# Split weights of the input projections: low part by a negation on GpSimd and an accumulating DMA in place of a subtraction

## The chip, the cores and the metric

The kernel runs on one core of a Trainium2 chip. It is one launch for both layers of a small model and two request groups. The metric is the device time of an execution in microseconds (us), taken as the median of several runs. Five engines work beside each other: TensorE (PE, matmuls, with PEld for the loads of its weights), VectorE (DVE), ScalarE (ACT), GpSimd (POOL) and SyncE (SP, which here only issues DMAs). Each runs its own list of instructions in order and waits on semaphores for the others; 16 DMA engines move data.

## The reference

Each of the two layers adds the output of three mixers and then a feed-forward part to x. All three mixers read slices of one combined projection `h @ w_in`, 1024 to 2600 columns.

```
def layer(x, ...):
    h = rms_norm(x, g_mix)
    z = h @ w_in                                   # 1024 x 2600
    za, zb, q, k, v, qi, ki, wi = split(z)
    y_a = u * (W_s v + b)       of gelu(za)        # mixer A: spatial gate over chunks of 128
    y_b = gb * conv3(gc * h_in) of zb              # mixer B: causal convolution of width 3
    y_c = attention over the top-k keys that the indexer (qi, ki, wi) picks   # mixer C
    x = x + concat(y_a, y_b, y_c) @ w_out
    hf = rms_norm(x, g_ffn)
    return x + relu(hf @ w_up) ** 2 @ w_down
```

Inputs are 512 rows of a new stream and 32 rows of a running one with 1024 cached keys, all in float32. Beside y, the new keys, values, indexer keys and states of the two request groups are outputs.

## The kernel before

**Products in three passes.** A float32 product is made of float32r matmuls, a format that PE takes in one pass. Every operand is split into a high part `hi` (the value rounded to float32r) and a low part `lo` (what is missing), and `mm3` adds hi x hi, hi x lo and lo x hi. For weights this is done by `load_w`, for activations by `split`.

**Loading weights.** `load_w` takes 1024 weight columns in a partition at a time (592 for the indexer): SP loads them as they are into `raw` (two buffers), ACT writes `hi` (line 216), and DVE or POOL writes `lo = raw - hi` (line 217). `hi` and `lo` lie in a ring of 3072 columns each, which is three blocks: the high part of a block can be written when PE has ended the block three before it. The engine for line 217 is DVE unless the caller names POOL with `nc.gpsimd`.

**The input projections.** In both layers the order in the source is: the indexer (line 353, 296 columns in four blocks), Q in two groups, K, V and mixer A's v (256 columns each, in two blocks: rows 0 to 511 and 512 to 1023 of the weights), then mixer A's u and mixer B's three groups (`w_feat`, 128 columns a block, two blocks each). The 256-column groups are products with tokens as output rows (`tok_gemm`): each of five token blocks has 24 matmuls, the first 12 with the group's first weight block, the last 12 with its second. For the first token block, line 377 also multiplies the sample's rows by `raw` itself. In the 128-column groups (`fm_gemm`) a weight block has two halves of 24 matmuls.

**Who sets the order.** A list scheduler turns the source into one list for each engine, by priorities (`prep` for weights, `evac` for copies out of PSUM) and its own idea of how long things take. So the same source lines come in another order when an operation changes. What lies beside the projections is work for DVE and ACT: rotary tables (lines 396 to 398), squares and norms (lines 596 to 648), the indexer's scores (lines 546 to 550), the search of the top-k (lines 405 to 456) and the softmax. Line 380 is ACT's copy of the sample's part product out of PSUM; line 644 begins the norm of a K block.

**POOL's list.** It holds the subtractions of the indexer's blocks of layer 1, of Q, V and mixer A's u, copies of the sample's normed rows (line 261), the tables of the next layer, the first three blocks of `w_up`, and the issues of small stores (line 511 indexer keys, 650 keys, 669 values).

Of the kernel before, what the change touches and what calls it, by code (L numbers as in the profile page):

```python
# [25 lines left out]
# column groups of w_in  # L26
# [5 lines left out]
# scheduling priorities of weight loads and of copies out of PSUM  # L32
PREP = -1000000
EVAC = -2000000
# columns of the ring of split weights
# [3 lines left out]
class Shift:  # L39
    """Shifts the scheduling priority of what is traced inside."""  # L40
# [12 lines left out]
def kernel(  # L53
# [45 lines left out]
    def tr(out, in_, ident):  # L99
        """A transpose on TensorE, which moves the bits as they are (float32r in one pass)."""  # L100
        if in_.dtype == F32R:
            out = out.bitcast(F32R)
        nc.tensor.transpose(out, in_, ident)  # L103
# [20 lines left out]
    # per-feature vectors as columns: g_mix, g_ffn, conv_w, state_conv  # L124
# [23 lines left out]
    def rsqrt_newton(r, s, scale, shape_like):  # L148
        """r = (s * scale) ** -0.5, the table's value with one Newton step; s may lie in PSUM."""
        r0 = shape_like()  # L150
        nc.scalar.activation(r0, s, AF.Abs_reciprocal_sqrt, scale=scale)
        u = shape_like()
        nc.vector.scalar_tensor_tensor(u, s, -0.5 * scale, r0, op0=ALU.mult, op1=ALU.mult)
        nc.vector.tensor_tensor(u, u, r0, op=ALU.mult)
        nc.vector.scalar_tensor_tensor(r, u, 1.5, r0, op0=ALU.add, op1=ALU.mult)
# [3 lines left out]
    def take_x(h, tags):  # L159
        """A half of x to feature-major, and the norm's factors along the rows' columns."""  # L160
        blocks = (0, 1) if h == 0 else (2, 3, 4)
        nb = len(blocks)
        size = lambda b: 128 if b < 4 else NS
        s, r = sm(nb, "sa", 6), sm(nb, "sa", 6)
        nc.vector.memset(s, 1.0)
        for i, b in enumerate(blocks):
            n = size(b)
            nc.scalar.activation(junk[:n, i % 2], xin[b][:n], AF.Square, accum_out=s[:n, i:i + 1])
        nc.vector.tensor_scalar(s, s, EPS * D, None, op0=ALU.add)
        rsqrt_newton(r, s, 1.0 / D, lambda: sm(nb, "sr"))  # L170
        rst[h] = T(HALF[h])
        pr = psum("d")
        for i, b in enumerate(blocks):
            n = size(b)
            for g in range(2):
                p = psum(next(tags))
                for k in range(4):
                    tr(p[:, k * n:k * n + n], xin[b][:n, (4 * g + k) * 128:(4 * g + k + 1) * 128], idn[:n, :n])
                dst = xs[h][:, 4 * g:4 * g + 4, i * 128:i * 128 + n]
                src = p[:, :4 * n].rearrange("p (k n) -> p k n", k=4)  # L180
                if g == 0:
                    nc.vector.tensor_copy(dst, src)
                else:
                    nc.scalar.copy(dst, src)
        for i, b in enumerate(blocks):
            n = size(b)
            dr = T(128, "tt")
            nc.vector.tensor_scalar(dr[:n, :n], idn[:n, :n], r[:n, i:i + 1], None, op0=ALU.mult)
            nc.tensor.matmul(pr[:, i * 128:i * 128 + n], lhsT=ones[:n, :], rhs=dr[:n, :n], start=True, stop=True)
        nc.vector.tensor_copy(rst[h], pr[:, :HALF[h]])  # L190
# [11 lines left out]
    ring = [wp.tile([128, RING], F32R, name="hi"), wp.tile([128, RING], F32R, name="lo"), 0]  # L202

    def load_w(fill, a, c, eng=None):
        """a row blocks of weights, c columns each: two float32r parts that sum to them exactly, and they themselves."""
        with prep:
            raw = rawp.tile([128, a, c], F32, tag="raw", name=nm("raw"))
            if callable(fill):
                fill(raw)
            else:  # L210
                nc.sync.dma_start(raw, fill.rearrange("(k p) c -> p k c", p=128))
            if ring[2] + a * c > RING:
                ring[2] = 0
            hi, lo = (t[:, ring[2]:ring[2] + a * c].rearrange("p (k c) -> p k c", k=a) for t in ring[:2])
            ring[2] += a * c
            nc.scalar.copy(hi, raw)  # L216
            (eng or nc.vector).tensor_tensor(lo, raw, hi.bitcast(F32), op=ALU.subtract)  # L217
        return [(hi[:, k], lo[:, k], raw[:, k]) for k in range(a)]
# [11 lines left out]
    # the sample's normed rows, not split  # L230
    hraw = const.tile([128, 8, 32], F32, name="hraw")

    def add_square(h, m):
        """Adds the squares of block m of x to the half's sum (with the eps share of a partition)."""
        n = HALF[h]
        t = T(n)
        nc.scalar.activation(t, xs[h][:, m, :], AF.Square)
        if m == 0:
            ssq[h] = keep([128, n], f"work{h + 1}")
            nc.vector.tensor_scalar(ssq[h], t, EPS * D / 128, None, op0=ALU.add)  # L240
        else:
            nc.vector.tensor_tensor(ssq[h], ssq[h], t, op=ALU.add)  # L242
# [21 lines left out]
    def results(b, g, tag):  # L264
        """A block's output, half of its features, back to token-major."""
# [15 lines left out]
    def prepare(l):  # L281
# [42 lines left out]
    def search_constants():  # L324
# [3 lines left out]
        # for the threshold search: prefix sums, the copies' total, steps  # L328
# [15 lines left out]
    for l in range(depth):  # L344
# [8 lines left out]
        idxw += w_tok(C_IDX, 296, ((2, 4), (4, 6), (6, 8)), nc.gpsimd if l else None)  # L353
# [11 lines left out]
        def tok_gemm(b, pieces, n, aside=True):  # L365
            """Token-major product of a block; aside: the sample's rows by themselves, in float32."""
# [5 lines left out]
            if b == 0 and aside:  # L372
                # the sample's rows: parts of the sum side by side in the array's columns
# [17 lines left out]
        def rope(t1, t2, x, ca, sb, half):  # L391
            """t1 = x * cos, t2 = swapped x * sin; x [rows, j, h, e] in PSUM."""
# [8 lines left out]
        def topk_mask(work, n, rounds, tag):  # L401
            """Turns scores into 0 where taken and NEG elsewhere."""
# [6 lines left out]
        def sample_mask(x):  # L409
            """The same for the sample's scores, whose rows are there four times (rows 32 j + t).  # L410

            The k-th largest score is found digit by digit (two bits of its float's exponent or mantissa at a
            time, each copy of a row trying one digit); equal scores are taken in the order of the keys.
            """
# [4 lines left out]
            # sign of the k-th largest; which one of sgn * x it is  # L419
# [7 lines left out]
            def digit(nb):  # L427
                """How many candidates of a row at least kk of sgn * x reach (a tie at the candidate counts half)."""
# [29 lines left out]
            # a tie at the last candidate may have hidden it: count exactly there  # L458
# [10 lines left out]
            # prefix counts of the equal ones  # L469
# [8 lines left out]
            # as many of them as are missing: k - (sum of signs + n - equal) / 2  # L478
# [15 lines left out]
        for b in range(5):  # L494
# [58 lines left out]
            else:  # L553
# [5 lines left out]
                # w as two [(head, t), (copy, t)] matrices  # L559
# [47 lines left out]
        for u in range(2):  # L607
            pieces = w_tok(C_Q + 256 * u, 256, ((0, 4), (4, 8)), nc.gpsimd)
            for b in range(5):
# [5 lines left out]
                # columns (j, hh, e) to (hh, j, e)  # L615
# [15 lines left out]
        pieces = w_tok(C_K, 256, ((0, 4), (4, 8)))  # L631
# [28 lines left out]
        pieces = w_tok(C_V, 256, ((0, 4), (4, 8)), nc.gpsimd)  # L660
# [18 lines left out]
        def attend(b):  # L679
            """The block's steps of a pair of query heads: scores and softmax, then the values."""  # L680
# [3 lines left out]
            def scores(u, hh):  # L684
                # two key heads side by side: their scores in halves of the array's rows
# [21 lines left out]
            def values(u, hh, probs, po):  # L707
                for k0 in range(0, b + 1, 2):
# [7 lines left out]
                    # and their values in halves of its columns  # L716
# [16 lines left out]
        def attend_sample():  # L733
# [17 lines left out]
            # queries, scaled  # L751
# [43 lines left out]
        def fm_gemm(h, src, ws, k0=0):  # L795
            """Feature-major product of a half: the weights' columns are the output's rows."""
            p = psum("m")
            n = HALF[h]
            for i, w in enumerate(ws):
                mm3(p[:, :n], w, (src[h][0][:, k0 + i, :], src[h][1][:, k0 + i, :]), i == 0, i == len(ws) - 1)  # L800
            return p
# [7 lines left out]
        def mixers():  # L809
# [1 line left out]
            mixT = [T(2 * n, "g").rearrange("p (h n) -> p h n", h=2) for n in HALF]  # L811
            pieces = w_tok(C_VA, 256, ((0, 4), (4, 8)))
# [27 lines left out]
            for fb in range(2):  # L840
                wt = w_feat(C_U + 128 * fb, nc.gpsimd)
# [8 lines left out]
            for fb in range(2):  # L850
                gc = T(NT + NS, "g")
                wt = w_feat(C_GC + 128 * fb)
# [9 lines left out]
                wt = w_feat(C_H + 128 * fb)  # L862
# [13 lines left out]
                wt = w_feat(C_GB + 128 * fb)  # L876
# [39 lines left out]
        def heat(h, m):  # L916
            """Has ScalarE's table for the norm loaded before its first use."""
# [70 lines left out]
def _constants():  # L988
    """Identity and rotary tables: they depend on shapes alone."""
# [13 lines left out]
    # the sum over the copies 1..3 of a row  # L1003
# [41 lines left out]
```

## Time and profile before

| | |
|---|---|
| three runs | 1397.32, 1400.68, 1401.14 us; median 1400.68 |
| span of the profiled execution (the page gives no other time of it) | 1403.4 us |
| mean granted TensorE clock | 0.982 |
| busy: PE / PEld / DVE / ACT / POOL | 1353.1 / 1265.8 / 840.0 / 615.9 / 115.3 us |
| weight blocks: high part on ACT | 188 |
| low part on DVE / on POOL | 163 / 25 |
| DMA bytes, mean rate | 113.00 MB, 81 GB/s |

The input projections and attention of layer 0 stand at 10 to 250 us of the span, those of layer 1 at 700 to 940 us. What lies after each is the output projection and the feed-forward part. An engine's busy time says little by itself here; the waits inside one stage are what is read.

### The profile page before, as it was taken

Reading aid. Unit: us, or ns where it says so; the run is one execution under the profiler, and the core shown is the slowest. Engines: PE = TensorE matmul, PEld = TensorE weight load, DVE = VectorE, ACT = ScalarE, POOL = GpSimd, SP = SyncE. Lnnn points to the kernel's source line nnn. Section 1 sums busy time; section 2 is a strip of 40 time slices with the busy share of each in tenths; the row PEclk is TensorE's granted clock in tenths of the full one; section 3 lists DMA queues with packets and bytes.
Section 4 is the critical chain, followed back from the end, with each engine's and each line's share of the span. In section 5 each row is a group of like instructions: output and inputs, shape, how many; then the busy total and the mean of one; then the engine's idle time right before and its main releaser. Section 6 shows DMA issues by size and latency. Waiting matters only on the chain. (4 is left out here: it accounts for less than half of the span.)

```text
span 1403.4 us, 25751 instructions
## 1 busy us (share of the span) xinstructions
PE 1353.1 (96%) x10430; PEld 1265.8 (90%) x10430; DVE 840.0 (60%) x2103; ACT 615.9 (44%) x1212; POOL 115.3 (8%) x125
## 2 busy tenths in 40 slices
PE   7998999998999999999989899999899999999998
PEld 5877886898999999999987789779799999999998
DVE  6999987468434334334489999865853343443442
ACT  5746996335314224223246489842542231331321
POOL 4414200010000000000042120000200000000000
PEclk8999999999999999999988999999999999999999
DMA  7124221323233332333212222222233332233322
GB/s 185 33 71 106 68 64 48 94 68 89 81 88 91 91 84 84 89 91 91 64 49 62 58 81 77 76 61 61 61 95 88 91 91 86 82 90 91 91 81 74
DMA packets 183566, 113.00 MB, mean 81 GB/s; under 512 B 7028, under 2 KB 180616, under 8 KB 183448
## 3 DMA queue, kind: packets, MB, share of 16 engines
q1 hardware_dynamic: 180808, 106.35, 26.2%
q0 software_dynamic: 2640, 5.01, 1.8%
q8 instruction: 82, 1.34, 0.4%
q14 instruction: 36, 0.29, 0.1%
HBM read 106.67 MB, written 4.67 MB: 79 GB/s over the span
## 5 line engine op out<-in xcount | busy, mean ns | idle before, releaser
L216 ACT CAST hi<-raw 128x1024 fp32r<-128x1024 f32 (+1 forms) x188 | 194.1, 1032 | 404.6 <-PE psm L226 389.1
L217 DVE TENSOR_TENSOR lo<-raw,hi 128x1024 fp32r<-128x1024 f32 (+1 forms) x163 | 197.5, 1212 | 174.9 <-ACT hi L216 174.2
L908 DVE TENSOR_TENSOR x<-x,psm 128x256 f32<-128x256 f32 (+1 forms) x192 | 83.7, 437 | 232.4 <-PE psm L227 232.0
L226 PE MATMUL psm<-h1lo,hi 128*128 128x288 f32 x640 | 190.4, 298 | 0.9 <-DVE h1lo L222 0.9
L227 PE MATMUL psm<-a1hi,lo 128*128 128x288 f32 x640 | 190.0, 297 | 0.0
L226 PE MATMUL psm<-a1lo,hi 128*128 128x288 f32 x640 | 189.9, 297 | 0.0
L225 PE MATMUL psm<-a1hi,hi 128*128 128x288 f32 x640 | 189.8, 297 | 0.0
L225 PE MATMUL psm<-h1hi,hi 128*128 128x288 f32 x640 | 188.7, 296 | 1.1 <-ACT h1hi L221 1.1
L227 PE MATMUL psm<-h1hi,lo 128*128 128x288 f32 x640 | 189.1, 296 | 0.0
L226 PE MATMUL psm<-h0lo,hi 128*128 128x256 f32 x640 | 181.9, 285 | 6.2 <-DVE h0lo L222 6.2
L225 PE MATMUL psm<-a0hi,hi 128*128 128x256 f32 x640 | 183.0, 286 | 0.0
L226 PE MATMUL psm<-a0lo,hi 128*128 128x256 f32 x640 | 182.0, 284 | 0.0
L227 PE MATMUL psm<-a0hi,lo 128*128 128x256 f32 x640 | 182.0, 284 | 0.0
L225 PE MATMUL psm<-h0hi,hi 128*128 128x256 f32 x640 | 181.4, 284 | 0.0
L227 PE MATMUL psm<-h0hi,lo 128*128 128x256 f32 x640 | 180.0, 282 | 0.0
L226 PEld LDWEIGHTS psm<-h0lo,hi 128*128 128x128 f32 x640 | 120.4, 188 | 8.6 <-DVE h0lo L222 7.1
L225 PEld LDWEIGHTS psm<-h1hi,hi 128*128 128x128 f32 x640 | 120.1, 188 | 2.7 <-ACT h1hi L221 1.5
L225 PEld LDWEIGHTS psm<-a0hi,hi 128*128 128x128 f32 x640 | 121.6, 190 | 0.5 <-issue 0.5
L226 PEld LDWEIGHTS psm<-h1lo,hi 128*128 128x128 f32 x640 | 120.3, 188 | 1.8 <-DVE h1lo L222 1.3
L226 PEld LDWEIGHTS psm<-a0lo,hi 128*128 128x128 f32 x640 | 121.2, 189 | 0.6 <-issue 0.5
L225 PEld LDWEIGHTS psm<-h0hi,hi 128*128 128x128 f32 x640 | 120.6, 189 | 1.2 <-issue 0.9
L227 PEld LDWEIGHTS psm<-a0hi,lo 128*128 128x128 f32 x640 | 121.6, 190 | 0.0
(318 smaller groups left out, 2841.1 us busy)
## 6 DMA issues: line engine op xcount, KB each, us to landing
raw<-in_w_up_dram SPq DMA_DIRECT2D x64, 512.0 KB, 4.1
raw<-in_w_down_dram SPq DMA_DIRECT2D x64, 512.0 KB, 3.9
raw<-in_w_in_dram SPq DMA_DIRECT2D x36, 512.0 KB, 3.9
raw<-in_w_out_dram SPq DMA_DIRECT2D x8, 512.0 KB, 3.8
raw<-in_w_out_dram SPq DMA_DIRECT2D x32, 128.0 KB, 3.0
raw<-in_w_in_dram SPq DMA_DIRECT2D x8, 296.0 KB, 6.1
q<-in_cache_k_dram SPq DMA_DIRECT2D x4, 512.0 KB, 4.3
h1lo<-in_cache_v_dram SPq DMA_DIRECT2D x2, 1024.0 KB, 7.1
```

Source lines behind the costliest of these rows:

```text
L216: nc.scalar.copy(hi, raw)
L217: (eng or nc.vector).tensor_tensor(lo, raw, hi.bitcast(F32), op=ALU.subtract)
L225: nc.tensor.matmul(out, lhsT=st[0], rhs=mv[0], start=first, stop=False)
L226: nc.tensor.matmul(out, lhsT=st[0], rhs=mv[1], start=False, stop=False)
L227: nc.tensor.matmul(out, lhsT=st[1], rhs=mv[0], start=False, stop=last)
L908: nc.vector.tensor_tensor(xs[h][:, m, :], xs[h][:, m, :], p[:, :HALF[h]], op=ALU.add)
```

## The change

For the input projections, the argument `eng` of `load_w` becomes the word "dma". Then POOL writes `lo = -hi`, and a DMA that POOL issues adds `raw` to what stands in `lo`. This is done for 39 blocks: in both layers Q (4), K, V and mixer A's v (2 each), u and mixer B's groups (8 in all), and in layer 1 the last three blocks of the indexer. Of these, 19 were subtracted on POOL and 20 on DVE before. The first layer's indexer, `w_out`, `w_up` and `w_down` stay as they are.

```
             hi, lo = (t[:, ring[2]:ring[2] + a * c].rearrange("p (k c) -> p k c", k=a) for t in ring[:2])
             ring[2] += a * c
             nc.scalar.copy(hi, raw)
-            (eng or nc.vector).tensor_tensor(lo, raw, hi.bitcast(F32), op=ALU.subtract)
+            if eng == "dma":
+
+                nc.gpsimd.tensor_scalar(lo, hi.bitcast(F32), -1.0, None, op0=ALU.mult)
+                nc.gpsimd.dma_start(lo, raw, accum_op=ALU.add)
+            else:
+                (eng or nc.vector).tensor_tensor(lo, raw, hi.bitcast(F32), op=ALU.subtract)
...
-        idxw += w_tok(C_IDX, 296, ((2, 4), (4, 6), (6, 8)), nc.gpsimd if l else None)
+        idxw += w_tok(C_IDX, 296, ((2, 4), (4, 6), (6, 8)), "dma" if l else None)
...
-            pieces = w_tok(C_Q + 256 * u, 256, ((0, 4), (4, 8)), nc.gpsimd)
+            pieces = w_tok(C_Q + 256 * u, 256, ((0, 4), (4, 8)), "dma")
...
-        pieces = w_tok(C_K, 256, ((0, 4), (4, 8)))
+        pieces = w_tok(C_K, 256, ((0, 4), (4, 8)), "dma")
...
-        pieces = w_tok(C_V, 256, ((0, 4), (4, 8)), nc.gpsimd)
+        pieces = w_tok(C_V, 256, ((0, 4), (4, 8)), "dma")
...
-            pieces = w_tok(C_VA, 256, ((0, 4), (4, 8)))
+            pieces = w_tok(C_VA, 256, ((0, 4), (4, 8)), "dma")
...
-                wt = w_feat(C_U + 128 * fb, nc.gpsimd)
+                wt = w_feat(C_U + 128 * fb, "dma")
...
-                wt = w_feat(C_GC + 128 * fb)
+                wt = w_feat(C_GC + 128 * fb, "dma")
...
-                wt = w_feat(C_H + 128 * fb)
+                wt = w_feat(C_H + 128 * fb, "dma")
...
-                wt = w_feat(C_GB + 128 * fb)
+                wt = w_feat(C_GB + 128 * fb, "dma")
```

The rest of the diff drops comments. Lines behind 217 have numbers higher by five after the change, so 226 becomes 231 and 511 becomes 516. The raw buffer of a block is now free when its accumulating DMA has landed.

POOL's list in layer 0 where Q begins, before: `raw_217_869` and `raw_218_873` are Q's first two blocks, `t_118_567` to `t_172_771` the indexer keys of token blocks 2 to 4.

```order
L217 TENSOR_TENSOR lo_163<-raw_217_869,hi_162 128x1024
L511 DMA out_4_dram<-t_118_567 128x32
L511 DMA out_4_dram<-t_145_669 128x32
L217 TENSOR_TENSOR lo_163<-raw_218_873,hi_162 128x1024
L513 DMA out_8_dram<-t_172_771 32x32
```

The same place of POOL's list after; `raw_218_874` is Q's second block, and a row `lo<-hi` is the negation of the block that the next DMA into `lo` adds.

```order
L219 TENSOR_SCALAR lo_163<-hi_162 128x1024
L516 DMA out_4_dram<-t_118_567 128x32
L220 DMA lo_163<-raw_217_869 128x1024
L219 TENSOR_SCALAR lo_163<-hi_162 128x1024
L516 DMA out_4_dram<-t_145_669 128x32
L220 DMA lo_163<-raw_218_874 128x1024
L518 DMA out_8_dram<-t_172_771 32x32
```

A block has two rows instead of one, and the issue of each add stands behind the store of an indexer key, of token block 2 for the first and 3 for the second.

PE's list at the same place before, from Q's first matmul to its first on a low part; line 544 is the indexer's score.

```order
L225 MATMUL psm_221_888<-hi_162,h0hi_28_184 128x256
L544 MATMUL psl_103_506<-kiTp_65_325,q_97_487 128x256
L226 MATMUL psm_221_888<-lo_163,h0hi_28_184 128x256
L544 MATMUL psl_107_516<-kiTp_65_325,q_97_487 128x256
L227 MATMUL psm_221_888<-hi_162,h0lo_29_185 128x256
```

And after:

```order
L230 MATMUL psm_221_890<-hi_162,h0hi_28_184 128x256
L549 MATMUL psl_103_506<-kiTp_65_325,q_97_487 128x256
L549 MATMUL psl_107_516<-kiTp_65_325,q_97_487 128x256
L230 MATMUL psm_225_924<-hi_162,h0hi_28_184 128x256
L230 MATMUL psm_229_958<-hi_162,h1hi_53_279 128x256
L549 MATMUL psl_109_521<-kiTp_65_325,q_97_487 128x256
L549 MATMUL psd_111_526<-kiTp_65_325,q_97_487 128x256
L549 MATMUL psl_113_531<-kiTp_65_325,q_97_487 128x256
L549 MATMUL psl_115_536<-kiTp_65_325,q_97_487 128x256
L231 MATMUL psm_221_890<-lo_163,h0hi_28_184 128x256
```

Eight matmuls stand between the first high and the first low part now, where one stood; among them the first matmuls of the next two token blocks.

PE's list in layer 0 where K's first token block (`psm_276`) comes from the first weight block to the second, before: the last of the first 12 matmuls, and the first two of the last 12.

```order
L227 MATMUL psm_276_1248<-hi_162,h0lo_29_185 128x256
L225 MATMUL psm_276_1248<-hi_162,h0hi_28_184 128x256
L226 MATMUL psm_276_1248<-lo_163,h0hi_28_184 128x256
L227 MATMUL psm_276_1248<-hi_162,h0lo_29_185 128x256
L225 MATMUL psm_276_1248<-hi_162,h0hi_28_184 128x256
```

And after; `psm_284` is the second token block:

```order
L230 MATMUL psm_276_1254<-hi_162,h0hi_28_184 128x256
L230 MATMUL psm_284_1300<-hi_162,h0hi_28_184 128x256
L231 MATMUL psm_284_1300<-lo_163,h0hi_28_184 128x256
L232 MATMUL psm_284_1300<-hi_162,h0lo_29_185 128x256
L230 MATMUL psm_284_1300<-hi_162,h0hi_28_184 128x256
L231 MATMUL psm_284_1300<-lo_163,h0hi_28_184 128x256
L232 MATMUL psm_284_1300<-hi_162,h0lo_29_185 128x256
L231 MATMUL psm_276_1254<-lo_163,h0hi_28_184 128x256
```

Six matmuls of the second token block, which need the first weight block alone, now stand ahead of the first use of the second block's low part.

## Rows read from the trace of the kernel before

**Rows 1.** Page, busy us of each engine, share of the span, instructions

```profile
PE 1353.1 (96%) x10430; PEld 1265.8 (90%) x10430; DVE 840.0 (60%) x2103; ACT 615.9 (44%) x1212; POOL 115.3 (8%) x125
```

**Rows 2.** Table by stage: start:end, length, busy us (instructions), clock, DMA share, GB/s

```profile
80.00:120.00 40.00, 35.97 (x274) 31.08 (x273) 37.53 (x131) 17.85 (x42) 8.54 (x9) 0.97 0.23 70
...
640.00:700.00 60.00, 60.00 (x479) 60.00 (x479) 27.38 (x51) 19.63 (x37) 0.00 (x0) 1.00 0.28 81
```

**Rows 3.** PE's waits, 40 to 200 us: total us, times, longest us

```profile
PE psm L225 <- ACT t L380: 2.9, 2, 2.4
PE psl L544 <- ACT t L546: 2.4, 1, 2.4
PE psx L103 <- DVE sr L644: 1.6, 1, 1.6
PE psl L103 <- ACT t L546: 1.4, 1, 1.4
```

**Rows 4.** PE's waits, 690 to 870 us

```profile
PE psm L225 <- ACT t L380: 2.8, 2, 2.3
PE psx L252 <- DVE work L242: 2.2, 1, 2.2
PE psl L544 <- ACT q L540: 2.0, 1, 2.0
PE psx L103 <- DVE sr L644: 2.0, 1, 2.0
PE psd L544 <- ACT t L546: 1.6, 1, 1.6
PE psl L103 <- DVE q L561: 1.1, 1, 1.1
```

**Rows 5.** Table by stage, a stretch at a granted clock of 0.50

```profile
118.01:121.42 3.41, 3.41 (x18) 3.41 (x18) 3.24 (x22) 2.40 (x4) 1.67 (x4) 0.50 0.41 136
```

**Rows 6.** Timeline of POOL, 103 to 118 us: start, us, instruction, [idle before]

```profile
112.38 2.37 POOL L217 TENSOR_TENSOR lo<-raw,hi 128x1024 fp32r<-128x1024 f32 x1
```

**Rows 7.** Timeline of DVE, 103 to 118 us

```profile
103.18 0.41 DVE L641 TENSOR_TENSOR t<-t,t 128x256 f32<-128x256 f32 x1
...
112.16 2.88 DVE L641 TENSOR_TENSOR t<-t,t 128x256 f32<-128x256 f32 x1
```

**Rows 8.** Groups of instructions, DVE: busy us, mean ns of one, idle before

```profile
L217 DVE TENSOR_TENSOR lo<-raw,hi 128x1024 fp32r<-128x1024 f32 (+1 forms) x163 | 197.5, 1212 | 174.9 <-ACT hi L216 174.2 <-DMA raw<-in_w_out_dram 0.5
```

**Rows 9.** Groups of instructions, POOL, shapes apart

```profile
L217 POOL TENSOR_TENSOR lo<-raw,hi 128x1024 fp32r<-128x1024 f32 x22 | 53.1, 2415 | 353.3 <-ACT hi L216 349.3 <-PE psl L103 3.9
...
L332 POOL CAST tri<-q 128x640 bf16<-128x640 f32 x1 | 0.8, 817 | 3.6 <-DMA q<-in_c_tri_dram 3.6
...
L338 POOL CAST idb<-idr 128x128 bf16<-128x128 f32 x1 | 0.3, 302 | 0.0
```

**Rows 10.** DMA issues: KB each, median us from issue to landing

```profile
raw<-in_w_down_dram SPq DMA_DIRECT2D x64, 512.0 KB, 3.9
...
h1lo<-in_cache_v_dram SPq DMA_DIRECT2D x2, 1024.0 KB, 7.1
...
out_dram<-t POOLq DMA_DIRECT2D x8, 128.0 KB, 2.0
```

**Rows 11.** Page, DMA queue: packets, MB, share of 16 engines

```profile
q1 hardware_dynamic: 180808, 106.35, 26.2%
```

**Rows 12.** Timeline of ACT, 93.5 to 101 us

```profile
95.98 1.03 ACT L216 CAST hi<-raw 128x1024 fp32r<-128x1024 f32 x1
```

**Rows 13.** Timeline of PE, 93.5 to 101 us

```profile
94.80 0.28 PE L227 MATMUL psm<-hi,h1lo 128*128 128x256 f32 x1
...
99.94 0.28 PE L226 MATMUL psm<-lo,h0hi 128*128 128x256 f32 x1
```

**Rows 14.** Timeline of POOL, 44 to 54 us

```profile
46.57 1.22 POOL L511 DMA_DIRECT2D out_dram<-t  x2
```

**Rows 15.** Timeline of PE, 46 to 53.5 us

```profile
47.27 0.28 PE L226 MATMUL psm<-lo,h0hi 128*128 128x256 f32 x1
```

## The prediction

> **What bounds the kernel now.** I read the page's busy times first, then the table by stage, then who waits for whom on TensorE (PE), then the timeline around the longest waits. The reader is to see in the first that PE is busy for 1353.1 us [rows 1], so all its idle time in a span of 1403.4 us is 50 us. The table by stage shows where that time isn't: in the feed-forward part PE is busy for 60.00 of 60 us and issues a matmul every 60/479 = 0.125 us, while at 80 to 120 us, in the input projections that the change touches, it has 35.97 of 40, with VectorE (DVE) at 37.53 [rows 2]. There DVE is the engine behind PE's waits, directly or through ScalarE (ACT): 2.4, 1.4, 1.6 and a 2.4 of the 2.9 in the first layer [rows 3], and 2.2, 2.0, 2.0, 1.6, 1.1 and most of 2.8 in the second [rows 4]. That is about 20 us over both layers, and it is nearly all that a change to these stages can win from waits. A gap also costs clock: after the wait that ends at 116.8 us PE has a granted clock of 0.50 for 3.41 us, that is the 1.2 GHz level [rows 5]. Such a window takes 3.41/2 = 1.7 us of PE's work, and there is one behind most of these waits.
>
> What makes DVE late is not its own subtractions but those of GpSimd (POOL). The timeline of DVE has one and the same instruction (line 641) at 0.41 us and at 2.88 us; the long one stands beside a subtraction on POOL that runs from 112.38 for 2.37 us [rows 6, 7]. DVE instructions on two SBUF operands stop while POOL subtracts. The waits of rows 3 and 4 follow such stops by 1 to 5 us.
>
> **The change part by part.** Changed are 39 blocks of input-projection weights: 18 in layer 0 and 21 in layer 1. 19 of them were subtracted on POOL, 20 on DVE. In a block two steps now stand where one stood: POOL writes the negated high part, and an accumulating DMA, issued by POOL, adds the raw block to it.
>
> *Removed from DVE:* 20 subtractions of 1.212 us [rows 8], 24 us. I cost this at nothing. In these stages each such block now gives DVE a hold by POOL's negation in exchange, and where PE is saturated (after 160 us of a layer) a faster DVE helps nobody.
>
> *On POOL:* the subtraction of 1024 columns takes 2.415 us, a one-input copy of 640 columns 0.817 and one of 128 columns 0.302 [rows 9]. So (0.817-0.302)/512 = 1.01 ns a column, and the negation is 0.302+896 x 1.01 ns = 1.21 us (estimate). The bounds are this and the two-input 2.415. I take 1.21, since the copies too have one input. A hold of DVE gets shorter by 2.37-1.21 = 1.16 us, if a one-input instruction holds DVE at all, which no row shows apart: the gain of a place lies between nothing (it holds as long as before) and 2.37 (it doesn't hold).
>
> The Trainium skill (SBUF — State Buffer, Who interferes with whom) says that a DVE instruction with two SBUF inputs contends with a GpSimd instruction that reads SBUF, and that the second to issue is blocked until the first ends. By this the trace agrees for the subtraction, and the negation, which reads SBUF, would hold DVE for its own length; so the page speaks for 1.16 and against 2.37.
>
> Of the waits in rows 3 and 4, seven shrink: 1.4, 1.6 and 2.4 (for line 380) in layer 0, 2.0 (for line 644), 2.3 (of the 2.8 for line 380), 1.6 and 1.1 in layer 1. Seven times 1.16, the last at its 1.1: -8.1 us. In layer 1 the three 592-column blocks of the indexer stood in the norm that PE waits for (2.2 [rows 4]); scaled by columns, 3 x 1.16 x 592/1024 = -2.0.
>
> *The new latency.* Today the low part is there one subtraction after the high part. Now it is: negation 1.2, semaphore 0.1, then issue to landing of an accumulating SBUF-to-SBUF DMA of 512 KB. No row has one. Loads of 512 KB land in 3.9 us and of 1024 KB in 7.1, and a store of 128 KB from POOL's queue in 2.0 [rows 10]. The bounds are 3.9 (as a plain copy) and 7.1 (it moves what 1024 KB move, since it has to read the old destination as well). In between: all hardware-queue packets moved 106.35 MB in 26.2% of 16 engines' span [rows 11], so an engine moves 106.35 MB/(0.262 x 16 x 1403.4 us) = 18 GB/s. A store of 128 KB has 8 KB an engine; two reads of 512 KB have 64 KB an engine, 56 KB or 3.1 us more, on top of 2.0: 5.1 us. I take 5.1 (estimate); it is nearer to 3.9.
>
> The Trainium skill (Collectives: The Full Stack, The bandwidth ceiling) says that an add inside a DMA engine is slow not for the add but because it needs two source reads, at half the rate of a copy. No run here shows it. [...]
>
> Where does that meet PE? The ring holds three blocks. In mixers and projections of 128 columns two blocks of 48 matmuls lie between a freed slot and the first use: 2 x 48 x 0.125 = 12 us, against 0.1 (semaphore)+1.05 (high part)+0.1+1.2+0.1+5.1 = 7.7. Covered; this cover is gone from a landing of 9.4 on. Later raw loads are covered in the same way, since a raw buffer is free 5 us later and the load itself takes 4 of those 12. Not covered are the second blocks of the 256-column groups. K in layer 0: the slot is freed at 95.08 (94.80+0.28), the high part is made from 95.98 to 97.01, the low part is first used at 99.94 [rows 12, 13]. Now: negation to 98.3, issue 98.4, landing 103.5. The new order puts the use some 0.7 us later (six matmuls of the next token block stand in between), 100.65. So PE waits 2.85 us, and again in layer 1, where the order is the same: +5.7. The second blocks of V and of mixer A have the wait for line 380 or some attention work in between, which makes them 2 to 3 us longer; I put +1.0 for the four.
>
> At the start of Q the accumulating DMA stands in POOL's queue behind the store of an indexer key. That store was issued at 46.57 [rows 14], held up by the subtraction; with 1.1 us less hold and 0.6 for the issue, the add is issued at 46.1 and lands at 51.2. PE used the low part at 47.27 [rows 15] and has eight matmuls put ahead of it, so it wants it at 48.6 and waits 2.6. The wait of 2.4 that stood 4 us later (layer 1: 2.0) goes in return, since DVE and ACT catch up meanwhile: +0.2 and +0.6, +0.8 in all. Behind the waiting add nothing stands on POOL that PE needs sooner.
>
> **Sum.** -8.1 -2.0 +5.7 +1.0 +0.8 = -2.6 us. Half-clock windows I leave at zero: two or three should go with the shorter waits, as many come with those at K and Q. The sum is made in the profiled execution, of which the page tells the span alone, 1403.4 us; the three runs have a median of 1400.68, 2.7 less, so I take the sum off that: 1398 us.
>
> **Rivals.** *The add is dear.* If it lands in 7.1 us or later (1024 KB did [rows 10]), the eight uncovered second blocks and Q starts wait 2.0 us longer each, +16, and four or so of them are then long enough for a half-clock window of 1.7 us of lost work: +4 to +25, about 1418, slower. It decides from a landing of 6 us on. For it: the operation reads twice and no row shows it. Against: rows of 4 KB in a partition, longer than those of the loads.
> *The add is as cheap as a plain copy, or the negation doesn't hold DVE.* At 3.9 us six places wait 1.2 less: -2.6-7.2 = -9.8, about 1391. A negation without a hold gives the same order of gain.
> *The negation is as slow as the subtraction.* Then -8.1 and -2.0 are gone and the chain grows by 1.2 at some six places: -2.6+10.1+7 = +14.5, about 1415. For it: nothing but that the operation is arithmetic and not a copy. Against: the copies' 1.01 ns a column.
> *It doesn't matter,* because the moved orders of PE and DVE fill the waits with other work: 1400.
>
> **How the numbers follow.** About 0.3% (4.2 us) is what a measurement of this kernel can tell from no change. The forecast has 0.47, own range 1392 to 1405: 0.17 faster, 0.28 same, 0.02 slower. The cheap add 0.20, faster. The dear add 0.21, slower. The slow negation 0.08, slower. No matter 0.04, same. Together faster 0.37, same 0.32, slower 0.31. The range 1387 to 1415 leaves out the far ends of the cheap and the dear add.
>
> **What would show it.** In the profile after: POOL's negation rows near 1.2 us with DVE instructions beside them at up to 1.6 us, not 2.9; 39 accumulating DMAs with a landing near 5; PE waits of 2 to 3 us for the DMA of a low part at Q's start and K's second block in both layers, and none in the mixers; the waits for lines 380 and 644 near 1 us. The prediction is wrong if the landing is under 4 or over 6, if the negation takes over 1.6 us, or if PE waits for low parts in the mixers.

## The result: 2.8% slower, and the profile after

The changed kernel takes 1439.66 us (median of four runs, 1434.98 to 1441.72), the kernel before 1400.91 in the same runs: a ratio of 1.0277, interval 1.0254 to 1.0300. Forecast were 1398 and a range of 1387 to 1415. The profiled execution has a span of 1436.6 us, 33.2 more than before.

The busy times on the page of the changed kernel, as in [rows 1]:

```profile
PE 1362.4 (95%) x10428; PEld 1272.0 (89%) x10430; DVE 807.5 (56%) x2083; ACT 613.5 (43%) x1210; POOL 211.9 (15%) x184
```

DVE is busy for 32.5 us less (24 are the 20 subtractions, the rest shorter holds), and POOL's time has nearly doubled. PE is busy for 9.3 us more with the same matmuls (most of it is clock, below) and idle for 24 us more. The groups of POOL, shapes apart, as in [rows 9]:

```profile
L219 POOL TENSOR_SCALAR lo<-hi 128x1024 fp32r<-128x1024 f32 x36 | 102.1, 2836 | 181.4 <-ACT hi L216 145.8 <-issue 35.5
L220 POOL DMA_DIRECT2D lo<-raw x39 | 36.1, 926 | 8.7 <-POOL lo L219 7.2 <-PE psm L232 0.6 <-PE psm L827 0.3
```

and the DMA issues (KB each, median us from issue to landing), as in [rows 10]:

```profile
raw<-in_w_in_dram SPq DMA_DIRECT2D x36, 512.0 KB, 3.6
lo<-raw POOLq DMA_DIRECT2D x36, 512.0 KB, 4.6
```

The add lands in 4.6 us, sooner than the 5.1 taken. The negation takes 2.84 us, not 1.21; it is slower than the two-input subtraction of 2.415 that stood as the upper bound.

What PE waits for at 40 to 210 us (us in total, times, longest), where [rows 3] has none of the first two rows:

```profile
PE psm L231 <- DMA lo<-raw: 6.9, 3, 3.4
PE pso L724 <- ACT t L720: 6.4, 1, 6.4
PE psl L549 <- ACT t L551: 4.6, 2, 3.4
...
PE psm L230 <- ACT t L385: 1.4, 1, 1.4
```

and at 690 to 890 us, as in [rows 4]:

```profile
PE psm L231 <- DMA lo<-raw: 10.8, 6, 3.3
PE psx L103 <- ACT t L706: 4.4, 1, 4.4
PE psl L103 <- ACT t L551: 2.1, 1, 2.1
```

The 24 us of idle time are 17.7 us of waits for an add (6.9 + 10.8), 10.8 us of two long waits for ACT (6.4 + 4.4), and -4.4 us for all the rest. With PE's 9.3 us of additional busy time that is 33.4; the spans differ by 33.2.

**The wait for an add,** where the prediction placed one, K's second block in layer 0. The timelines of ACT, POOL and PE (start, us, instruction, [idle before]), as in [rows 12, 13]:

```profile
95.33 1.04 ACT L216 CAST hi<-raw 128x1024 fp32r<-128x1024 f32 x1
...
96.47 2.77 POOL L219 TENSOR_SCALAR lo<-hi 128x1024 fp32r<-128x1024 f32 x1 [6.75 <-ACT hi L216]
99.53 0.89 POOL L220 DMA_DIRECT2D lo<-raw  x1 [0.30 <-POOL lo L219]
...
104.81 0.39 PE L231 MATMUL psm<-lo,h0hi 128*128 128x256 f32 x1 [3.38 <-DMA lo<-raw]
```

The high part is ready at 96.4, the low part at 104.8: 0.1 + 2.77 + 0.3 + 5.2 (this add's issue to landing) = 8.4 us. Before, it was ready 2.5 us after the high part. PE stands for 3.38 us, and behind it comes a stretch at the 1.2 GHz level in which it does half its work (table by stage, the column with 0.50 is the granted clock), as in [rows 5]:

```profile
106.03:109.44 3.41, 3.41 (x19) 3.41 (x18) 1.94 (x7) 0.38 (x1) 1.56 (x2) 0.50 0.84 212
```

Not all nine waits for an add have just this chain. Before four of them the negation itself begins 0.9 to 3.4 us late, behind other work in POOL's list. The longest delay is at mixer A's second block in layer 0, whose high part is ready at 134.28 (timeline of POOL):

```profile
135.78 0.86 POOL L297 TENSOR_TENSOR tab<-tab,t 128x320 f32<-128x320 f32 x1 [4.07 <-DMA t<-in_q_gain_dram]
...
137.71 2.80 POOL L219 TENSOR_SCALAR lo<-hi 128x1024 fp32r<-128x1024 f32 x1
```

POOL stands in the tables of the next layer, which wait for their own load; the low part is ready at 146.9, 12.6 us after the high part. Before, this block was subtracted on DVE.

**The long wait for ACT.** The timelines of SP's queue, ACT and PE at 171 to 180 us, where the mixers' blocks of 128 columns are loaded:

```profile
171.31 3.36 SPq L211 DMA_DIRECT2D raw<-in_w_in_dram  x2
...
178.28 1.04 ACT L216 CAST hi<-raw 128x1024 fp32r<-128x1024 f32 x1 [6.66 <-DMA raw<-in_w_in_dram]
179.23 0.36 ACT L720 COPY t<-psx 128x256 f32<-128x256 f32 x1
...
179.65 0.69 PE L724 MATMUL pso<-t,Vp 128*64 128x128 f32 x4 [6.42 <-ACT t L720]
```

The raw buffer is free only when its add has landed, at 171.25 for an add issued at 165.13. The load begins then and lands 6.9 us later, beside the next add and another load, where the median of these loads is 3.6. ACT waits for it, and a small copy of the softmax, which has nothing to do with the weights, stands behind it in ACT's list. PE waits for that copy. The wait of 4.4 us for line 706 in layer 1 has the same form; that load is issued 0.6 us after an add and takes 8.0 us.

**The hold of DVE** became shorter where the prediction read it. Timelines of POOL and DVE, as in [rows 6, 7]; line 646 is line 641 of before:

```profile
116.57 2.79 POOL L219 TENSOR_SCALAR lo<-hi 128x1024 fp32r<-128x1024 f32 x1
...
116.84 1.07 DVE L646 TENSOR_TENSOR t<-t,t 128x256 f32<-128x256 f32 x1
```

The instruction takes 1.07 us beside a negation, 2.88 beside a subtraction and 0.41 alone. Over the whole run 27 DVE instructions beside negations are lengthened by 20.3 us in all, by 0.6 as a median; before, 19 beside the subtractions of these blocks by 27.9 (each instruction's time less the lower quartile of the same instruction over all runs, where that is above 0.2 us, so that instructions held one behind the other count each; the subtractions of `w_up`, the same in both kernels, add 11.6 us in six).

At Q's start in layer 0 the hold became longer. The timelines of DVE, ACT and PE at 43 to 50 us:

```profile
44.32 4.20 DVE L553 TENSOR_SCALAR work<-t,wi 128x256 f32<-128x256 f32 x1
...
48.61 0.38 ACT L551 ACTIVATE t<-psl 128x256 f32<-128x256 f32 x1 [3.36 <-DVE work L553]
...
49.05 0.58 PE L549 MATMUL psl<-kiTp,q 128*128 128x256 f32 x1 [3.36 <-ACT t L551]
```

and the same DVE instruction before:

```profile
50.54 0.35 DVE L548 TENSOR_SCALAR work<-t,wi 128x256 f32<-128x256 f32 x1
```

Beside these 4.20 us POOL issues a store and an add, makes a negation (45.08 to 48.24) and issues the next store. Which of them holds DVE, these rows don't tell. PE's wait of 3.4 us for line 549 stands behind it. The first low part of Q lands in the meantime, at 49.09, so no wait for an add shows here.

### The profile page after: what moved, and what is told of

Its sections match the earlier page's. It is cut to its first block, busy times and chain, and to the rows that moved or that the text cites. A ratio compares the mean times of both kernels' runs of the same rounds, so it can differ in the third digit from the quotient of the medians.

```text
span 1436.6 us, 25861 instructions
## 1 busy us (share of the span) xinstructions
PE 1362.4 (95%) x10428; PEld 1272.0 (89%) x10430; DVE 807.5 (56%) x2083; ACT 613.5 (43%) x1210; POOL 211.9 (15%) x184
## 5 line engine op out<-in xcount | busy, mean ns | idle before, releaser
L222 DVE TENSOR_TENSOR lo<-raw,hi 128x1024 fp32r<-128x1024 f32 (+1 forms) x143 | 173.1, 1211 | 177.4 <-ACT hi L216 176.9
L219 POOL TENSOR_SCALAR lo<-hi 128x1024 fp32r<-128x1024 f32 (+1 forms) x39 | 107.7, 2762 | 572.9 <-DVE t L263 386.5
L230 PE MATMUL psm<-h0hi,hi 128*128 128x256 f32 x640 | 184.3, 288 | 0.0
L232 PEld LDWEIGHTS psm<-h0hi,lo 128*128 128x128 f32 x640 | 122.9, 193 | 1.3 <-issue 1.0
```

The lines of the kernel that those rows point to most:

```text
L219: nc.gpsimd.tensor_scalar(lo, hi.bitcast(F32), -1.0, None, op0=ALU.mult)
L230: nc.tensor.matmul(out, lhsT=st[0], rhs=mv[0], start=first, stop=False)
L232: nc.tensor.matmul(out, lhsT=st[1], rhs=mv[0], start=False, stop=last)
```

## The experiments

Theories: A, the loss is the long way from the high part to the usable low part, with the raw buffer held for it. B, it is GpSimd's slow negation and its hold of VectorE. Each edit is shown against the changed kernel; ratios are to the kernel before. The scheduler makes a new order for each kernel, except where the text says that the order stayed.

**1. Negation on VectorE.**

```
-                nc.gpsimd.tensor_scalar(lo, hi.bitcast(F32), -1.0, None, op0=ALU.mult)
+                nc.vector.tensor_scalar(lo, hi.bitcast(F32), -1.0, None, op0=ALU.mult)
```

> The 39 negations go from GpSimd (2.76 us each) to VectorE, the accumulating DMA stays. Theory A (the loss is the time from the high part to the usable low part, and the raw buffer that is held for it): of the chain of 0.1 + 2.77 + 0.3 + 4.6 = 7.8 us only the negation gets shorter, by some 1.5 to 2; the nine waits for an add keep about half of their 17.7 us, the waits behind blocked loads partly stay: 1412 to 1424. Theory B (the loss is GpSimd's slow negation and its hold of VectorE): all of it goes, 1390 to 1403.

1416.32 us, 1.0119 (1.0099 to 1.0139). The same negation on DVE:

```profile
L219 DVE TENSOR_SCALAR lo<-hi 128x1024 fp32r<-128x1024 f32 x36 | 24.7, 687 | 10.4 <-ACT hi L216 10.2
```

2.1 us less on the chain, and no hold, are worth 23 us; 16 us of loss stay with the add. As A had it, but it doesn't say whether the hold had a part.

**2. Add on VectorE.** The negation stays, no DMA.

```
-                nc.gpsimd.dma_start(lo, raw, accum_op=ALU.add)
+                nc.vector.tensor_tensor(lo, raw, lo.bitcast(F32), op=ALU.add)
```

> GpSimd's negation stays as it is, VectorE adds the raw block in place of the DMA. A: chain 2.77 + 0.1 + 1.2 = 4.1 us and the raw buffer is free after it, so nearly all waits for low parts and blocked loads go: 1400 to 1410. B: the negation and its holds are unchanged: 1425 to 1440.

1435.95 us, 1.0268 (1.0243 to 1.0292): A's number failed, and the time lies in B's range. But the edit brought a wait of its own. DVE's group of these adds (busy, mean, idle before):

```profile
L220 DVE TENSOR_TENSOR lo<-raw,lo 128x1024 fp32r<-128x1024 f32 x36 | 45.7, 1268 | 33.5 <-POOL lo L219 33.3
```

DVE's list stands for 33.3 us behind POOL's negations, and everything else on DVE with it. It tells that a slow link hurts on a busy engine too, and does not part A from B.

**3. The add reads the block from HBM again,** so the raw buffer is free early.

```
-                nc.gpsimd.dma_start(lo, raw, accum_op=ALU.add)
+                nc.gpsimd.dma_start(lo, fill.rearrange("(k p) c -> p k c", p=128), accum_op=ALU.add)
```

> Negation and accumulating DMA stay, but the DMA reads the block from HBM a second time, so that the raw buffer is free when the high part is made. A: the nine direct waits for an add (17.7 us) stay, the waits behind ScalarE blocked on a late raw load (6.4 and 4.4 us, with their half-clock windows) go: 1420 to 1430. B, and A without the part on the raw buffer: unchanged, 1435 to 1442. If reading from HBM lands later than from SBUF, the direct waits grow and it could pass 1442.

1444.53 us, 1.0310 (1.0282 to 1.0337). Landing, and PE's largest waits at 40 to 250 us:

```profile
lo<-in_w_in_dram POOLq DMA_DIRECT2D x36, 512.0 KB, 6.3
```

```profile
PE psm L231 <- DMA lo<-in_w_in_dram: 24.4, 5, 6.2
PE psm L230 <- ACT t L601: 1.2, 1, 1.2
```

The two long waits for ACT (lines 720 and 706) are gone, as A said. The add lands 1.7 us later, and the direct waits grow from 17.7 to 45 us (24.4 + 20.6 in layer 1). The one ate the other.

**4. All 39 blocks subtracted on VectorE.**

```
-                nc.gpsimd.tensor_scalar(lo, hi.bitcast(F32), -1.0, None, op0=ALU.mult)
-                nc.gpsimd.dma_start(lo, raw, accum_op=ALU.add)
+                nc.vector.tensor_tensor(lo, raw, hi.bitcast(F32), op=ALU.subtract)
```

> All 39 blocks are subtracted on VectorE: no GpSimd in the chain, no DMA. Chain 1.2 us. A and B: no slower than the kernel before, 1385 to 1401; if GpSimd's holds of VectorE made the waits of the kernel before, as the prediction read them, below 1392; if VectorE's own load made them, 1400 to 1410.

1394.42 us, 0.9966 (0.9950 to 0.9982). The 19 subtractions that come to DVE, some 22 us of work, cost nothing, and PE's waits in all fall from 45.9 to 39.1 us. So the holds seem to have made waits in the kernel before, though for 6 us and not for the 9 or more that "below 1392" asked; the order moved too, and the chain of these 19 blocks is 1.2 us shorter, though PE waited for no low part of theirs before.

**5. All 39 blocks subtracted on GpSimd.** 

```
-                nc.gpsimd.tensor_scalar(lo, hi.bitcast(F32), -1.0, None, op0=ALU.mult)
-                nc.gpsimd.dma_start(lo, raw, accum_op=ALU.add)
+                nc.gpsimd.tensor_tensor(lo, raw, hi.bitcast(F32), op=ALU.subtract)
```

> All 39 blocks are subtracted on GpSimd (2.41 us each), no DMA. If only the length of the chain counts (A): 0.1 + 2.4 = 2.5 us, shorter than K's slack of 2.9, so little over the kernel before: 1398 to 1406. If GpSimd's hold of VectorE for the whole of each subtraction counts (B): 20 more holds of up to 2.4 us, most of them in the projection stages: 1408 to 1425.

1434.97 us, 1.0236 (1.0212 to 1.0260): beyond both. The timelines of DVE and POOL:

```profile
810.89 2.87 DVE L645 TENSOR_TENSOR t<-t,t 128x256 f32<-128x256 f32 x1
...
811.11 2.37 POOL L219 TENSOR_TENSOR lo<-raw,hi 128x1024 fp32r<-128x1024 f32 x1
```

There is no add here and the chain is 2.5 us, 1.2 longer than in 4; but 31 DVE instructions beside the 39 subtractions are lengthened by 49.1 us, and by the ratios 38 us are lost against 4. PE waits for no low part of a weight block here; it waits longer for DVE and ACT. So holds can cost this much. That doesn't make them the cause of the change's whole loss, since there they sum to 20.3 us, less than before the change.

**6. Only the 16 blocks of the mixers by negation and add.** The other 23 as before.

```
-        idxw += w_tok(C_IDX, 296, ((2, 4), (4, 6), (6, 8)), "dma" if l else None)
+        idxw += w_tok(C_IDX, 296, ((2, 4), (4, 6), (6, 8)), nc.gpsimd if l else None)
-            pieces = w_tok(C_Q + 256 * u, 256, ((0, 4), (4, 8)), "dma")
+            pieces = w_tok(C_Q + 256 * u, 256, ((0, 4), (4, 8)), nc.gpsimd)
-        pieces = w_tok(C_K, 256, ((0, 4), (4, 8)), "dma")
+        pieces = w_tok(C_K, 256, ((0, 4), (4, 8)))
...
```

> Only the 16 blocks of 128 columns (u and mixer B) go by negation and accumulating DMA; the indexer, Q, K, V and mixer A's v as before. If the raw buffer held for the add counts (A): the two waits behind a blocked high part (6.4 and 4.4 us) and their half-clock windows stay, 1406 to 1416. If the 12 us between a free slot and the first use cover all, as the prediction had it: 1397 to 1404.

1419.72 us, 1.0127 (1.0105 to 1.0150), above A's range too. No wait of PE for an add is left here; what stands out is behind ACT (its timeline at 155 to 167 us):

```profile
164.78 1.04 ACT L216 CAST hi<-raw 128x1024 fp32r<-128x1024 f32 x1 [3.74 <-DMA raw<-in_w_in_dram]
165.74 0.40 ACT L706 ACTIVATE t<-t,sa 128x128 f32<-128x128 f32 x1
```

The load was issued at 157.5, 0.6 us behind an add, and took 7.2 us. PE's waits for line 706 are 8.4 us at 40 to 950 us, of 12.7 by which its waits in all grow. So "covered in the mixers" is true of the low parts and false of the raw buffers.

**7. Only the 23 other blocks by negation and add.** The mixers as before.

```
-                wt = w_feat(C_U + 128 * fb, "dma")
+                wt = w_feat(C_U + 128 * fb, nc.gpsimd)
-                wt = w_feat(C_GC + 128 * fb, "dma")
+                wt = w_feat(C_GC + 128 * fb)
...
```

> Only the 23 blocks of the indexer, Q, K, V and mixer A's v go by negation and accumulating DMA; u and mixer B as before. A: the nine waits for an add (17.7 us) and their clock stay, 1418 to 1432. With the run before it the two excesses over the kernel before should add up to about 39 us, if the parts are independent of each other.

1423.78 us, 1.0162 (1.0136 to 1.0189). PE's waits for adds are 18.3 us (6.9 + 11.4). The two excesses, 16.7 and 20.8, add up to 37.5 of 39: the parts are nearly independent.

**8 and 14. A plain copy by the DMA.** All engines keep the order of the changed kernel.

```
-                nc.gpsimd.dma_start(lo, raw, accum_op=ALU.add)
+                nc.gpsimd.dma_start(lo.bitcast(F32), raw)
```

> The DMA copies the raw block into the low part and leaves out the add, so the low parts are wrong by the high part; only its landing is looked at. If a second read of 512 KB makes the landing (the doubling that the prediction cited): 4.6 falls to 3.0 to 3.5 us. If latency and the write make it: 4.3 to 4.7.

> The plain copy by DMA once more, timed: it leaves out the add, all else and the order are as in the changed kernel. Landing 2.95 in place of 4.59 us, issue 0.58 in place of 0.93. If landing sets the loss: 1403 to 1411, as in the single look; if that look was chance: above 1425.

The low parts are wrong in both. A single run of 8: 1407.01 us; six runs of 14: 1413.83, 1.0082 (1.0064 to 1.0100), a little above what was expected. DMA issues of 14:

```profile
lo<-raw POOLq DMA_DIRECT2D x36, 512.0 KB, 3.0
```

1.6 us less to land and 0.35 less to issue give back 26 us of 39, with nothing else changed. PE's waits for the DMA fall from 17.7 to 10.9 us.

**9. Negation from the raw block,** without waiting for ACT.

```
-                nc.gpsimd.tensor_scalar(lo, hi.bitcast(F32), -1.0, None, op0=ALU.mult)
+                nc.gpsimd.tensor_scalar(lo, raw, -1.0, None, op0=ALU.mult)
```

> GpSimd makes the negation from the raw block instead of from the high part, so it need not wait for ScalarE's 1.05 us; its length, its holds of VectorE and the DMA stay. If the length of the chain sets the loss: it is some 1.1 us shorter, and by the copy's 33 us for 2 us that is worth 10 to 20: 1418 to 1430. If GpSimd's work itself does (holds): unchanged, 1434 to 1444.

1443.85 us, 1.0303 (1.0282 to 1.0323). It looks like B, but the order moved: at K's second block PE comes to the low part 5.0 us after the start of the high part, where it was 6.1, and that add took 6.8 us to land, not 5.2. What the chain lost, the scheduler had already given away. It tells nothing of the cause, and was the reason for tests with the order held.

**10 and 11. A third raw buffer,** with its control. Both have one buffer less of two kinds of temporaries.

```
-    rawp = ctx.enter_context(tc.tile_pool(name="rawp", bufs=2))
+    rawp = ctx.enter_context(tc.tile_pool(name="rawp", bufs=3))
```

> Control for the next run: two kinds of temporary tiles have one buffer less (tt 3, g 2), so that a third raw buffer fits; the change is otherwise as it is. Near the changed kernel: 1436 to 1448.

> As the control, with a third raw buffer. If the raw buffer that is held until the add has landed is a cause (theory A's second part, 10.8 us of waits behind blocked high parts and their clock): 10 to 20 below the control, and no wait for line 720 or 706 of 4 us or more. If the direct waits alone are the cause: within 4 of the control.

Control 1439.95 us, 1.0283 (1.0262 to 1.0303); third buffer 1436.39, 1.0252 (1.0232 to 1.0273). The 3.6 us between them are "within 4 of the control", the outcome that was to speak for the direct waits alone. But neither kernel kept the order. PE's waits for adds are 29.5 us in the control and 24.8 with the third buffer, where the changed kernel has 17.7, and of the long waits for lines 720 and 706 the control has only the second (3.8 us). The third buffer takes it away, and waits of 3.6 and 3.7 us for line 701 (DVE) stand elsewhere. What the held buffer costs in the changed kernel's own order, the pair doesn't tell.

**12. No subtraction on GpSimd at all,** as 4, and the first blocks of `w_up` on VectorE too.

```
-                    ws.append(load_w(w_up[l, :, c0:c0 + 128], 8, 128, nc.gpsimd if c == 0 and f < 3 else None))
+                    ws.append(load_w(w_up[l, :, c0:c0 + 128], 8, 128, None))
```

> All subtractions on VectorE, those of the first w_up blocks too (lines 247 and 263 were held there for 2.4 us each); no GpSimd subtraction is left. If the holds made the waits at the feed-forward's start (1.6, 1.3 and 1.8 us in each layer): 1382 to 1391. If VectorE's own load makes them: 1392 to 1396, as with VectorE for the 39 blocks alone.

1388.77 us, 0.9921 (0.9904 to 0.9937), faster than both kernels. PE's waits at 300 to 335 us, 5.6 us in the kernel before:

```profile
PE psm L229 <- ACT h1hi L225: 2.3, 1, 2.3
PE psm L231 <- DVE lo L221: 0.2, 1, 0.2
```

**13. A copy on GpSimd in place of the negation.** The order of all engines stayed.

```
-                nc.gpsimd.tensor_scalar(lo, hi.bitcast(F32), -1.0, None, op0=ALU.mult)
+                nc.gpsimd.tensor_copy(lo, hi.bitcast(F32))
```

> GpSimd copies the high part into the low part in place of negating it (so the add makes twice the high part; the sign is what is left out). All engines keep the order of the changed kernel. If a copy of 1024 columns takes the 1.2 us that the prediction worked out from the copies: the chain is 1.6 us shorter, as in the plain copy by DMA, and the time falls to 1403 to 1415; if GpSimd's hold of VectorE counts beside the chain, to below 1403. If the copy takes as long as the negation, the float32r output and not the arithmetic sets its length, and the time stays at 1434 to 1442.

1410.52 us, 1.0067 (1.0054 to 1.0080). POOL's group:

```profile
L219 POOL CAST lo<-hi 128x1024 fp32r<-128x1024 f32 x36 | 39.6, 1101 | 207.6 <-ACT hi L216 172.1 <-issue 35.5
```

The copy takes 1.10 us, near the 1.21 that the prediction worked out. So neither the input count nor the float32r output makes the negation slow, but its kind. 29 us of 39 go with 1.7 us. The direct waits hardly fall, 17.7 to 17.0. What goes are 11.3 us of waits for ACT (those for lines 720 and 706 from 10.8 to 3.0, those for line 551 from 6.7 to 1.8), 1.8 us of waits for DVE, and 13.7 us of PE's busy time. DVE instructions beside these copies are lengthened by 6.4 us in place of 20.3; line 553 takes 0.35.

**15. Both, copy and plain DMA,** order held.

> Both at once (a copy in place of the negation, a plain DMA in place of the add), order unchanged. If the loss is a chain longer than the slack, it falls off once the slack is reached: 1390 to 1402, much less than twice the gain of one. If the two gains add up, 1375 or lower. If the copy takes as long as the negation: as the plain copy alone, 1403 to 1411.

1393.64 us, 0.9945 (0.9926 to 0.9964). PE's waits for the DMA are 4.1 us. The two gains are 29 and 26 alone and 46 together, not 55: past a chain of 0.1 + 1.1 + 0.3 + 3.0 = 4.5 us little is left to gain. Experiment 4, with no DMA at all, is as fast (1394.42).

## Why the prediction was wrong

**The negation's duration** is the step that failed first and most. The prediction worked it out from copies and set the two-input subtraction as the upper bound; it is 2.84 us, past that bound. Experiment 13 puts the predicted size in its place with all lists held, and 29 of the 39 us go. The time is then 1410.5, still 12 us above the forecast, so this step is not the only one that failed. The rival "the negation is as slow as the subtraction" named the right operation. It had a chance of 0.08, with "nothing but that the operation is arithmetic" for it, and its price of 1415 was too low by 25 us, since it counted neither clock nor blocked loads. In the Trainium skill (GPSIMD Engine Reference, Engine selection) one-input work on GpSimd is called roughly line-rate. The copy's 1.10 us may pass as that; the negation, with one input, takes four times the 0.69 us of VectorE.

**The landing** was sized well: 5.1 taken, 4.6 measured as a median, and 5.2 at K. The add costs 1.6 us over a copy of the same bytes (4.6 against 3.0); that this is a second read fits and is not shown by itself. Eight of the 39 adds took 5.9 to 7.7 us. The three longest, 6.8, 6.9 and 7.7, were issued within 0.7 us of a 512 KB raw load; for others this is not explained.

**The waits at K** were right in place and nearly in size: 2.85 predicted, 3.38 and 3.33 measured. The sum for direct waits was 7.5, after what Q was to give back, and is 17.7: V's and mixer A's second blocks have 5.4 in place of 1.0, Q's blocks of layer 1 have 2.2, and the indexer's blocks of layer 1 wait for adds (2.6 and 0.8) where a gain of 2.0 was put down. At K this is the chain, 1.6 us longer by the negation. At mixer A's and Q's blocks POOL's list adds to it: what stands on POOL ahead of a negation was not counted.

**"Later raw loads are covered in the same way"** failed. The cover was counted for the low part's user, PE, and not for the engine that waits for the load. ACT's list is in order, so a load that is late by a landing stops whatever stands behind the high part. The load itself was taken as 4 us; the two behind the long waits took 6.9 and 8.0, the one in experiment 6 took 7.2. These waits were 10.8 us in the profile, and experiment 6 has them with no wait for an add (8.4 us; the time is 16.7 us longer). How much of the loss they make in the changed kernel's own order is not shown.

**The shrinking waits** were to give 10.1 us; all waits but those for an add and the two long ones for ACT gave 4.4. The waits for line 385 (380 before) and line 649 (644) shrank or went, others (lines 575, 601, 701) came. The wait of 2.4 us at Q's start in layer 0, which was to go since DVE and ACT catch up, became 3.4, behind the hold of line 553. That a hold gets shorter by 1.16 us was wrong in its reason (the negation is longer than the subtraction) and right in its direction at most places: line 646 loses 0.65 us, not 2.47; line 553 loses 3.85 where it lost nothing. In the Trainium skill (SBUF — State Buffer, Who interferes with whom) the second to issue is blocked until the first ends. The subtractions agree; beside the negation of 116.57 to 119.36 line 646 was done at 117.91.

**Clock windows "left at zero"** make most of the 9.3 us of PE's additional busy time. Summed over all stretches with a granted clock of 0.50, PE is busy there for 58.4 us after and 43.1 before; half of the difference, 7.6 us, is what they take. The three waits of 3.3 and 3.4 us (lines 549 and 231 in layer 0, 231 in layer 1) each have a stretch at the 1.2 GHz level (granted clock 0.50) beside or right behind them. In experiment 13 the 58.4 us are 22.1, and PE's busy time is 13.7 us lower with the same matmuls.

What stays open: how the negation's 29 us divide between chain and hold. The direct waits hardly moved in 13, which speaks for hold and blocked lists, and at line 553 the hold is seen, but both get shorter there. Experiment 14 leaves the negation as it is and shortens the rest of the chain by 2.0 us, and 26 us go; so the chain can make most of the loss by itself, but DVE's lengthening beside the negations falls there too, from 20.3 to 14.9 us. No run with the order held moved the one without the other.

## What to carry to other kernels

Measure an operation's duration on its engine in its own form: a bound from a neighbouring form (two inputs, a copy) isn't a bound. When a step becomes a chain over a DMA, count for each buffer on it who waits for the buffer and what stands behind that waiter in its in-order list, not the last user alone. And with a scheduler in between, trust an experiment on one link only if the order of all lists stayed; a shorter chain in a new order can read as no gain.

## What was not expected of the hardware

On GpSimd, 1024 columns of float32 to float32r take 1.10 us as a copy, 2.41 as a two-input subtraction and 2.84 as a multiplication by a constant; VectorE does that last one in 0.69. A multiplication by a constant on GpSimd mostly holds VectorE for less than its length (0.6 us as a median of 27 instructions), a subtraction up to all of it; but one VectorE instruction of 0.35 us took 4.20 beside a multiplication of 3.16 and three DMA issues of GpSimd. An accumulating DMA of 512 KB within SBUF lands in 4.6 us and holds its issuer for 0.93, a plain one in 3.0 and 0.58; the same add with its source in HBM lands in 6.3. Three 512 KB loads from HBM issued 0.6 to 2.2 us behind such an add took 6.9 to 8.0 us, where their median is 3.6.
